# Float32 products in place of fp32r products of exact parts, in a two-layer attention and expert kernel

## The chip, the cores and the metric

One core of one Trainium2 chip. The metric is the device time of one execution in microseconds (us), as a median of runs. Nothing is computed on the host; weights lie in HBM as float32.

## The reference

Two layers over 256 latent tokens and 256 context tokens of width 1024, all in float32. Each layer mixes tokens, then sends them through experts:

```python
h = modulate(x, sh1, sc1); hc = modulate(xc, csh1, csc1)     # adaLN: shift, scale from SiLU(c) @ w_ada
p = h @ w_in[l]                     # 1440 columns: q rank 384 | kv rank 256 | rotary key 32 | GLU 512 | pool 256
q = rms_norm(p_q) @ w_uq            # 8 heads of 64 + 32
k, v = rms_norm(p_kv) @ w_ukv
attn = softmax(q k^T) v             # latent queries see context and latent keys
conv = silu(layer_norm(conv31(glu(p_conv)))); pool = window means @ pool_w
x = layer_norm(alpha * x + g1 * (concat(attn, conv, pool) @ w_out[l]))
combine = top-1 of 4 groups, then top-2 of its 8 experts     # 32 experts
for e in range(32):
    y += combine[:, e] * ((silu(h2 @ w_gate[e]) * (h2 @ w_up[e])) @ w_down[e])
x = layer_norm(alpha * x + g2 * y)
```

The second layer does not update the context tokens, so there half of the tokens go through mixing and experts (`nq`, `nb` = 2 tiles of 128 tokens instead of 4).

## The kernel before

The kernel is written on a tile framework. For VectorE (V), ScalarE (S, ACT in the profile), GpSimd (G, POOL) and the DMA queue on SyncE (SP) the framework's planner puts the instructions in an order, from their priority in the program and its own estimate of durations; some places are pinned by hand (`tc.issue_after(instruction)`, `tc.high_priority`). In the expert loops TensorE's order is as written (`manual_schedule`).

**Weights.** `plan` lists every weight transfer in the order of use. `pump` (L175) issues the next one on SP's queue as soon as a place of 1 MB is free. `RING` = 6 places are there from the start; others are added as buffers fall free (`slot`): in layer 0 one tile `w` and four `c` tiles at the start of the experts (L1508, L1740), in layer 1 the second half of the tokens, two `early` tiles, `k2`, two `c` tiles, two `w` tiles, `cr` and `misc`.

**Exact parts.** Outside attention's scores and the expert weights, products run on fp32r. To keep accuracy both sides are split into a high part (rounded to fp32r) and a low part (what the rounding left), and three products are added: high x high, high x low, low x high. `wsplit` (L386) makes the parts of a weight in one of two `w` buffers: a copy on ACT (L395), a subtraction on VectorE or, where `SPG` says so, POOL (L401). `mm3` (L406) and L465 to L467, L793, L807 to L809 do the triples. Tokens are split in `tokens_T` (L446, L447) and L525 to L537, the normed low ranks in `rms_T` (L714, L715), the pieces of the mix at L763, L866, L952.

**Mixing** (`mixing`, L369). Layer 0 has 512 columns of tokens, layer 1 has 256. `proj_block` (L461) makes one of six blocks of 128 channels with eight triples. `lowrank` (L666) makes q and kv ranks, in layer 0 already with plain float32 products (L674), in layer 1 with triples of 288 and 384 columns. The convolution is 31 taps for each of two blocks on VectorE (L607), part of the second block on ACT and POOL (`conv_part`). `rms_T` squares on ACT, takes the root on POOL (L262), scales on VectorE (L703) and turns the result on TensorE (L711). `k_pair`, `q_pair` and the value product follow, then eight heads: scores L884 (float32), softmax, turns L919, values L941. The output projection `out_part` (L958) runs in four parts, halves of columns by halves of channels, each with 4 channel blocks for each token tile; `merge`, `stats`, `rows_T` and `logits` (L1095) follow, then the router on VectorE (L1204 to L1276). `exact` (L1159) writes the tokens to DRAM for the gathers and splits them (L1170, L1171).

**Experts** (`moe`, L1306). 16 pairs of experts in quads of two pairs; each expert takes up to 64 tokens. `slots` (L1345) finds which token is in which place. `gather` brings the tokens of a quad: for the first quad a product of the tokens' two parts with the one-hot table (L1396), for the others an indirect DMA and turns (L1392). `half` (L1416) multiplies gate and up for the two experts of a pair side by side on 64 columns of the array each, in plain float32; `hidden` (L1424 to L1426) the gate; `down` (L1460) the output, also float32. `weighted` (L1448) scales it and splits it into `O`'s two parts (L1450, L1451). `scatter` (L1465) brings two pairs back to one tile of tokens and one half of the columns, a *unit*: four fp32r products with the table `gt` (L1474), the gate (L1477), the sum on POOL or VectorE (L1478). The units of a quad are spread over the next quad's loop. A branch (`tc.If`, L1608) holds passes for experts with more than 64 tokens; layer 1 has one such pass built in (`one_pass`). Ahead of the branch in layer 0 two rows are scaled on POOL (L1506).

## Time and profile before

| what | value |
|---|---|
| median of 3 runs | 1072.38 us (1064.46 to 1073.56) |
| profiled execution, its own time | 1077.6 us |
| its span, first to last instruction | 1075.9 us |
| mean granted TensorE clock | 0.939 of full speed |
| read from HBM | 309.03 MB |

Stretches are given in us from the span's start. Layer 0 mixes until about 263, routes until about 332 and runs its experts until 600; layer 1 mixes until about 737, projects and routes until 802 and runs its experts to the end. PE is TensorE, DVE VectorE. A record of a matmul has a start and a modelled end that overlaps the next one, so the cost of one is read from start to start. A float32 product leaves two records in the trace, an fp32r product one.

### The profile page before, as it was taken

The page shows a single profiled execution, that of the slowest core. Times are in us where ns is not written, and L with a number is a line of the kernel's source. Part 1 is how long each engine was busy: PE and PEld are TensorE (multiplying, and loading weights), DVE is VectorE, ACT ScalarE, POOL GpSimd, SP SyncE. Part 2 cuts the span into 40 slices and gives each one's busy share as a digit, 9 for nine tenths or more (in the row PEclk, how much of TensorE's full clock was granted, in tenths as well). Part 3 has the DMA queues.
Part 4 walks back from the last instruction along what each step waited for, and adds up shares of the span by engine and source line. Part 5 has one row for each costly group of instructions (what it writes and reads, how often), then busy time and mean ns, then how long its engine had stood idle before and what let it go on. Part 6 is the DMA issues. An engine that isn't in the chain of part 4 may idle for free. (4 is left out here: it accounts for less than half of the span.)

```text
span 1075.9 us, 13982 instructions
## 1 busy us (share of the span) xinstructions
PE 952.6 (89%) x5153; PEld 553.3 (51%) x5153; DVE 604.5 (56%) x1157; ACT 303.6 (28%) x598; POOL 317.2 (29%) x280
## 2 busy tenths in 40 slices
PE   4996999999668999999999888898859997999994
PEld 2674586687543454445444687646633443443442
DVE  2599567757844344455344899877572333433336
ACT  2432365532401111111111536443212221221211
POOL 2334510002361334324234632102070122123222
PEclk8898899999888999999999999999769998998997
DMA  9844225865979999999998677265768999999971
GB/s 356 324 157 161 80 79 204 326 120 178 348 263 318 329 395 406 402 376 380 381 400 320 217 236 256 99 240 178 270 207 302 396 387 392 393 400 407 381 250 41
DMA packets 95530, 305.41 MB, mean 284 GB/s; under 512 B 10247, under 2 KB 30727, under 8 KB 87392
## 3 DMA queue, kind: packets, MB, share of 16 engines
q1 hardware_dynamic: 89744, 293.77, 74.9%
q0 software_dynamic: 4272, 6.14, 1.7%
q10 hardware_dynamic: 1440, 4.54, 1.1%
q8 instruction: 43, 0.70, 0.3%
q14 instruction: 31, 0.25, 0.1%
HBM read 309.03 MB, written 4.72 MB: 292 GB/s over the span
## 5 line engine op out<-in xcount | busy, mean ns | idle before, releaser
L1478 POOL TENSOR_TENSOR x<-x,tm 128x512 f32<-128x512 f32 x96 | 122.8, 1298 | 309.5 <-DVE tm L1477 309.1
L1416 PE MATMUL gu<-ring,xt 128*64 128x512 f32 x504 | 172.8, 624 | 0.0
L1416 PE MATMUL gu<-slot,xt 128*64 128x512 f32 x416 | 133.6, 612 | 0.0
L1451 DVE SCALAR_TENSOR_TENSOR O<-d,iw,O 128x512 fp32r<-128x512 f32 x63 | 47.2, 749 | 123.8 <-ACT O L1450 122.8
L1474 PE MATMUL y<-O,gt 128*128 128x512 f32 (+2 forms) x400 | 110.1, 412 | 4.2 <-DVE tm L1477 3.4
L1474 PEld LDWEIGHTS y<-O,gt 128*128 128x128 f32 (+1 forms) x400 | 70.7, 192 | 51.3 <-issue 25.9
L1477 DVE TENSOR_TENSOR tm<-y,lnb 128x512 f32<-128x512 f32 (+1 forms) x102 | 68.9, 677 | 46.3 <-PE y L1474 44.8
L1416 PEld LDWEIGHTS gu<-ring,xt 128*64 128x64 f32 x504 | 49.7, 143 | 67.9 <-issue 63.7
L1450 ACT ACTIVATE O<-d,iw 128x512 fp32r<-128x512 f32 x63 | 43.3, 688 | 140.5 <-PE d L1460 139.5
L1460 PE MATMUL d<-ring,ht 128*64 128x512 f32 x264 | 82.7, 597 | 0.2 <-DMA ring<-in_w_down_dram 0.2
L607 DVE SCALAR_TENSOR_TENSOR c0b<-c0a,hw,c0b 128x256 f32<-128x256 f32 (+1 forms) x105 | 73.6, 747 | 0.6
L1425 DVE SCALAR_TENSOR_TENSOR hd<-th,gu 128x256 f32<-128x256 f32 x32 | 13.5, 421 | 91.4 <-ACT th L1424 91.1
L1416 PEld LDWEIGHTS gu<-slot,xt 128*64 128x64 f32 x416 | 38.5, 140 | 50.9 <-issue 47.5
L395 ACT ACTIVATE w<-ring 128x1024 fp32r<-128x1024 f32 (+2 forms) x42 | 41.0, 978 | 66.4 <-PE p L409 47.4
L1460 PE MATMUL d<-slot,ht 128*64 128x512 f32 x168 | 52.7, 595 | 0.0
L401 DVE TENSOR_TENSOR w<-ring,w 128x1024 fp32r<-128x1024 f32 (+2 forms) x33 | 39.7, 1205 | 22.1 <-ACT w L395 21.9
L1375 POOL DMA_INDIRECT xg<-h2d,ix x28 | 32.9, 1174 | 52.6 <-DVE ix L1374 24.4
L296 PE MATMUL p<-ring,scw 128*32 128x256 f32 x672 | 45.1, 404 | 2.3 <-DMA ring<-in_w_ada_dram 2.3
L1424 ACT ACTIVATE th<-gu 128x256 f32<-128x256 f32 x32 | 12.3, 385 | 108.8 <-PE gu L1416 108.8
L408 PE MATMUL p<-w,mix 128*128 128x512 f32 x96 | 38.6, 402 | 4.9 <-DVE w L401 4.9
L1460 PEld LDWEIGHTS d<-ring,ht 128*64 128x64 f32 x264 | 24.2, 137 | 33.6 <-issue 31.1
L1392 PEld LDWEIGHTS x<-ident,xg 128*128 128x128 f32 x224 | 29.5, 192 | 21.2 <-issue 18.7
(424 smaller groups left out, 1876.5 us busy)
## 6 DMA issues: line engine op xcount, KB each, us to landing
ring<-in_w_ada_dram SPq DMA_DIRECT2D x46, 1024.0 KB, 7.7
ring<-in_w_down_dram SPq DMA_DIRECT2D x32, 1024.0 KB, 11.6
ring<-in_w_gate_dram SPq DMA_DIRECT2D x63, 512.0 KB, 13.3
ring<-in_w_up_dram SPq DMA_DIRECT2D x63, 512.0 KB, 9.9
slot<-in_w_gate_dram SPq DMA_DIRECT2D x54, 512.0 KB, 13.0
slot<-in_w_up_dram SPq DMA_DIRECT2D x54, 512.0 KB, 12.8
slot<-in_w_down_dram SPq DMA_DIRECT2D x21, 1024.0 KB, 14.8
ring<-in_w_in_dram SPq DMA_DIRECT2D x6, 1024.0 KB, 15.6
```

The lines of the kernel that those rows point to most:

```text
L296: T.matmul(ps[32 * q:32 * q + 32, :256], scw[:, j, 6 - 2 * k:38 - 2 * k], w[:, jj, q * 256:q * 256 + 256], start=(j == 0), stop=(j == 7), ...
L395: kept_hi.append(S.activation(h_, src, AF.Copy))
L401: ins = e.tensor_tensor(l_, src, h_.bitcast(FT), op=OP.subtract)
L408: T.matmul(ps, lh, rl, start=False, stop=False, skip_group_check=True)
L607: V.scalar_tensor_tensor(acc, tap(b, k), hw[:, b, k:k + 1], acc, op0=OP.mult, op1=OP.add)
L1416: T.matmul(gu[64 * s:64 * s + 64, :].rearrange("p (g c) -> p g c", g=2), xt[h][:, j % 4, o0 + 64 * s:o0 + 64 * s + 64], ws[s].rearrange("p ...
L1450: S.activation(oh, ps, AF.Copy, scale=w)
L1451: V.scalar_tensor_tensor(ol, ps, w, oh.bitcast(FT), op0=OP.mult, op1=OP.subtract)
L1460: T.matmul(ps[64 * s:64 * s + 64, :n], ht[:, k, 64 * s:64 * s + 64], ws(s, k, c, n), start=(k == 0), stop=(k == 1), skip_group_check=True, ...
L1474: T.matmul(ps, GT[key][r, t * 128:(t + 1) * 128], O[key][k][r, c], start=(i == 0 and k == 0), stop=(i == m - 1 and k == 1))
L1477: V.tensor_tensor(tm, ps, gates[t // 2][hf][:, c0:c0 + n], op=OP.mult)
L1478: eng.tensor_tensor(x[:, t, cols], x[:, t, cols], tm, op=OP.add)
```

## The change

All fp32r tiles become float32 tiles and every triple, and every pair with a split side, becomes one float32 product. `wsplit`, `mm3`, `proj_w` and all low parts go; weights are read where the DMA put them, and a place is given back when the products on it are done. The key product runs as two 64-column halves side by side. The scaled tokens of layer 0 are made on ACT and VectorE in turn; every second low-rank piece is scaled on VectorE. The pins of `mixes(1)`, `conv_part` and of the late splits go. `RING` is 8; in layer 0 two `c` tiles become places already after attention and two more with the experts; layer 1 gets one `early` tile, and `c0a` at the experts, but no `w` tile. The scaling at L1506 moves from POOL to ACT. `info` has four columns instead of six.

```diff
-RING = 6
+RING = 8
...
-            def wsplit(src, n, eng=None, late=0):
...
-            def mm3(ps, lh, ll, rh, rl, start, stop):
-                T.matmul(ps, lh, rh, start=start, stop=False, skip_group_check=True)
-                T.matmul(ps, lh, rl, start=False, stop=False, skip_group_check=True)
-                T.matmul(ps, ll, rh, start=False, stop=stop, skip_group_check=True)
...
-                    T.matmul(ps[:, :NQ], wh[:, j, :], hTh[j][:, :NQ], start=(j == 0), stop=False)
-                    T.matmul(ps[:, :NQ], wh[:, j, :], hTl[j][:, :NQ], start=False, stop=False)
-                    T.matmul(ps[:, :NQ], wl[:, j, :], hTh[j][:, :NQ], start=False, stop=(j == 7))
+                    T.matmul(ps[:, :NQ], src[:, j, c * 128:(c + 1) * 128], hT[j][:, :NQ], start=(j == 0), stop=(j == 7))
...
-            with tc.issue_after(kept_lo[0].ins):
-                mixes(1)
-            with tc.issue_after(kept_hi[-CP].ins) if CP else nullcontext():
-                conv_part(1, 0, CONV1[l])
+            mixes(1)
+            conv_part(1, 0, CONV1[l])
...
-                    for n, (x1, x2) in enumerate(((wkh, kT[j][0]), (wkh, kT[j][1]), (wkl, kT[j][0]))):
-                        T.matmul(ps, x1[:, j, cols], x2, start=(j == 0 and n == 0), stop=(j == 1 and n == 2))
+                    for e in range(2):
+                        T.matmul(ps[64 * e:64 * e + 64, :], w[:, j, 2 * hp + e, 0:64], kT[j], start=(j == 0), stop=(j == 1),
+                                 skip_group_check=True, tile_position=(0, 64 * e))
...
-                        mm3(ops[hf][t], mixh[b][:, t * 128:(t + 1) * 128], mixl[b][:, t * 128:(t + 1) * 128],
-                            wh[:, k, :], wl[:, k, :], bi == 0 and b2 == 0 and k == 0,
-                            bi == 1 and b2 == 1 and k == 1)
+                    T.matmul(ops[hf][t], mix[4 * bb + k][:, t * 128:(t + 1) * 128], w[:, k, :],
+                             start=(bi == 0 and k == 0), stop=(bi == 1 and k == 3), skip_group_check=True)
...
-                S.activation(hh, h2, AF.Copy)
-                (G if t % 2 else V).tensor_tensor(hl, h2, hh.bitcast(FT), op=OP.subtract)
...
-                        for k, h2 in enumerate((h2h, h2l)):
-                            T.matmul(ps[:, jj * 256:jj * 256 + n], h2[t][:, 128 * j:128 * j + 128], g[:, t, :n],
-                                     start=(t == 0 and k == 0), stop=(t == nb - 1 and k == 1), skip_group_check=True)
+                        T.matmul(ps[:, jj * 256:jj * 256 + n], h2[t][:, j::8], g[:, t, :n],
+                                 start=(t == 0), stop=(t == nb - 1), skip_group_check=True)
...
-                S.activation(oh, ps, AF.Copy, scale=w)
-                V.scalar_tensor_tensor(ol, ps, w, oh.bitcast(FT), op0=OP.mult, op1=OP.subtract)
+                S.activation(o, ps, AF.Copy, scale=IW[key][:, 6:7])
...
-                        for k in range(2):
-                            r, c = (slice(0, 128), cols) if key != "o" else (slice(64 * hf, 64 * hf + 64), slice(0, 512))
-                            T.matmul(ps, GT[key][r, t * 128:(t + 1) * 128], O[key][k][r, c],
-                                     start=(i == 0 and k == 0), stop=(i == m - 1 and k == 1))
+                        r, c = (slice(0, 128), cols) if key != "o" else (slice(64 * hf, 64 * hf + 64), slice(0, 512))
+                        T.matmul(ps, GT[key][r, t * 128:(t + 1) * 128], O[key][r, c], start=(i == 0), stop=(i == m - 1))
...
-                    G.tensor_scalar(t_, t_, ALPHA, None, op0=OP.mult)
+                    S.activation(t_, t_, AF.Copy, scale=ALPHA)
```

## Rows read from the trace of the kernel before

**Rows 1.** The page, busy time of each engine, share, instructions.

```profile
PE 952.6 (89%) x5153; PEld 553.3 (51%) x5153; DVE 604.5 (56%) x1157; ACT 303.6 (28%) x598; POOL 317.2 (29%) x280
```

**Rows 2.** Stretches: length, busy time of five engines, PE clock, DMA share, GB/s.

```profile
0.00:130.00 130.00, 101.48 (x604) 69.14 (x605) 83.84 (x116) 41.79 (x85) 51.90 (x54) 0.89 0.59 215
130.00:263.00 133.00, 132.54 (x800) 97.34 (x799) 89.49 (x183) 60.87 (x132) 8.71 (x10) 1.00 0.58 184
263.00:332.00 69.00, 46.32 (x369) 31.76 (x369) 47.26 (x83) 17.48 (x24) 37.09 (x27) 0.83 0.86 307
332.00:600.00 268.00, 256.88 (x1230) 121.61 (x1227) 116.88 (x215) 44.83 (x90) 95.95 (x80) 1.00 0.99 371
600.00:737.00 137.00, 122.24 (x790) 94.09 (x788) 117.40 (x227) 68.40 (x135) 34.87 (x30) 0.96 0.59 202
737.00:802.00 65.00, 45.31 (x242) 32.81 (x241) 45.60 (x105) 14.11 (x18) 24.91 (x27) 0.76 0.70 226
802.00:1076.00 274.00, 247.80 (x1128) 106.55 (x1128) 104.04 (x230) 56.12 (x117) 63.73 (x55) 0.93 0.86 329
```

**Rows 3.** PE's waits, 332 to 600 us: total, times, longest.

```profile
PE y L1432 <- DVE hd L1426: 7.5, 6, 1.3
PE y L1432 <- DMA slot<-in_w_up_dram: 1.2, 1, 1.2
```

**Rows 4.** PE's waits, 0 to 130, 263 to 332, 600 to 802, 802 on.

```profile
PE p L711 <- DVE t L703: 12.2, 1, 12.2
...
PE y L1345 <- PEq L1608: 5.5, 1, 5.5
PE p L1235 <- DVE t L1229: 4.7, 1, 4.7
...
PE p L408 <- DVE w L401: 8.8, 5, 4.9
PE y L1345 <- DVEq L1608: 8.6, 1, 8.6
...
PE x L1396 <- DVE t L1263: 3.6, 1, 3.6
...
PE x L1387 <- DMA xo<-h2d,ix: 5.7, 1, 5.7
```

**Rows 5.** PE's timeline (start, length, what), scores of head 0.

```profile
162.49 1.88 PE L884 MATMUL p<-c1b,c0b 128*128 128x512 f32 x4
164.20 1.03 PE L889 MATMUL p<-c1b,c0b 128*128 128x256 f32 x4
```

**Rows 6.** PE's timeline, output projection of layer 0, first product and what follows.

```profile
229.88 0.48 PE L407 MATMUL p<-w,mix 128*128 128x512 f32 x1
...
262.89 1.95 PE L1084 MATMUL p<-ident,x 128*128 128x128 f32 x16
```

**Rows 7.** PE's timeline, two scatter units and what follows.

```profile
368.42 2.10 PE L1474 MATMUL y<-O,gt 128*128 128x512 f32 x8
370.46 3.65 PE L1416 MATMUL gu<-slot,xt 128*64 128x512 f32 x16
```

**Rows 8.** PE's timeline, second half of the first gather.

```profile
302.19 4.10 PE L1396 MATMUL x<-g,h 128*128 128x256 f32 x32
306.12 0.95 PE L1345 MATMUL y<-info,g 128*128 128x6 f32 x8
```

**Rows 9.** DVE's timeline ahead of L703.

```profile
98.41 2.35 DVE L401 TENSOR_TENSOR w<-ring,w 128x1024 fp32r<-128x1024 f32 x2
100.68 6.70 DVE L607 SCALAR_TENSOR_TENSOR c0b<-c0a,hw,c0b 128x512 f32<-128x512 f32 x10
```

**Rows 10.** Timelines of DVE and POOL around the routers and the branch.

```profile
285.81 1.99 DVE L1171 TENSOR_TENSOR h<-hn,h 128x1024 fp32r<-128x1024 f32 x1
...
305.70 5.93 POOL L1506 TENSOR_SCALAR lnb<-lnb 128x1024 f32<-128x1024 f32 x2 [7.92 <-DMA lnb<-in_rpack_dram]
...
779.69 2.97 DVE L1247 TENSOR_TENSOR g<-iot,pos 128x512 fp32r<-128x512 f32 x1
```

More of the change, by code (lines that the diff above doesn't have):

```diff
@@ L1 @@
 import math
-from contextlib import ExitStack, nullcontext
+from contextlib import ExitStack
 import concourse.bass as bass
@@ L265, in big @@
     def big(tag, shape, dt, name):
-        return per.tile(shape, dt, tag=tag, name=name, bufs=2 if tag == "w" else 1)
+        return per.tile(shape, dt, tag=tag, name=name)
     def blocks(tags, n, m, dt, name):
@@ L472, in mixing @@
             if l == 0:
-                kt2 = big("k2", [128, 4, 512], FT, "xT")
-                xT = [kt2[:, k, :] for k in range(4)] + [cv1[0][:, 1152:1664], cv1[1][:, 1088:1600], cv0[1][:, 512:1024], t2(FT)]
+                xT = blocks("k2 w", 8, 512, FT, "xT")
                 for j in range(8):
@@ L830, in mixing @@
                 conv(1)
-                mixh[4:6], mixl[4:6] = (blocks(b, 2, NQ, FR, "mix") for b in ("b0d", "b1d"))
             cst = sb.tile([128, 4, 6], FT, tag="cst", name="cst")
@@ L963, in out_part @@
                 w = get(("out", l, hf, bb))
-                parts = [wsplit(w[:, 2 * b2:2 * b2 + 2, :], 1024, V, LATE[l] if hf + bi == 0 else 0) for b2 in range(2)]
-                order = [(b2, t) for b2 in range(2) for t in range(nq)]
+                order = [(k, t) for k in range(4) for t in range(nq)]
                 if hf == 1 and bi == 1:
-                    order = [(b2, t) for t in range(nq) for b2 in range(2)]
-                for b2, t in order:
-                    if each and b2 == 0:
+                    order = [(k, t) for t in range(nq) for k in range(4)]
+                for k, t in order:
+                    if each and k == 0:
                         each(t)
-                    wh, wl = parts[b2]
-                    for k in range(2):
-                        b = 4 * bb + 2 * b2 + k
-                        mm3(ops[hf][t], mixh[b][:, t * 128:(t + 1) * 128], mixl[b][:, t * 128:(t + 1) * 128],
-                            wh[:, k, :], wl[:, k, :], bi == 0 and b2 == 0 and k == 0,
-                            bi == 1 and b2 == 1 and k == 1)
+                    T.matmul(ops[hf][t], mix[4 * bb + k][:, t * 128:(t + 1) * 128], w[:, k, :],
+                             start=(bi == 0 and k == 0), stop=(bi == 1 and k == 3), skip_group_check=True)
                 done(("out", l, hf, bb))
@@ L1051, in mixing @@
                         e.tensor_tensor(xs, xs, lg_[1][hf], op=OP.add)
+            else:
+                held_.extend(big(c, [128, 2048], FT, "slot") for c in ("c1a", "c1b"))
+                for t_ in held_:
+                    slot(t_)
             gate = [bc_row(dA, G1 + s) for s in range(ns)]
@@ L1133, in mixing @@
             if l:
-                for k in range(2):
-                    slot(big("w", [128, 2048], FT, "slot"))
-            if l:
                 behind(nq)
@@ L1505, in moe @@
                     row_to_all(t_, a["rpack"][l, :, 2, :], r, 0, 4)
-                    G.tensor_scalar(t_, t_, ALPHA, None, op0=OP.mult)
-            if not last:
-                more_ = [big("w", [128, 2048], FT, "slot")]
-                slot(more_[0])
+                    S.activation(t_, t_, AF.Copy, scale=ALPHA)
             def hot(q):
@@ L1731, in moe @@
                 one_pass()
-            if last:
-                XG = big("c0a", [128, 2, D], FT, "xg")
-                XG = [XG[:, k, :] for k in range(2)]
-                kept["xo"] = big("c1a", [128, D], FT, "xo")[0:64, :]
-                G.memset(kept["xo"], 0.0)
-            else:
-                XG = [big(b, [128, D], FT, "xg") for b in ("b0b", "b1b")]
-                more_ += [big(c, [128, 2048], FT, "slot") for c in ("c0a", "c0b", "c1a", "c1b")]
-                for t_ in more_[1:]:
-                    slot(t_)
+            XG = big("c1a" if last else "b0a", [128, 2, D], FT, "xg")
+            XG = [XG[:, k, :] for k in range(2)]
             for k in range(2):
                 G.memset(XG[k], 0.0)
-            ohs, ols = (blocks(b, 3, D, FR, "O") for b in ("b0d b0a", "b1d b1a"))
+            if last:
+                kept["xo"] = big("b1b", [128, D], FT, "xo")[0:64, :]
+                G.memset(kept["xo"], 0.0)
+                slot(big("c0a", [128, 2048], FT, "slot"))
+            else:
+                held_.extend(big(c, [128, 2048], FT, "slot") for c in ("c0a", "c0b"))
+                for t_ in held_[2:]:
+                    slot(t_)
+            os_ = blocks("b0d b1d b0b", 3, D, FT, "O")
             order.enter_context(tc.manual_schedule(engines={mybir.EngineType.PE}))
@@ L1793, in moe @@
                     done(("wd", l, e))
[L1794 removed]
+                O[i] = o_
                 if not odd:
```

239 lines of the change are left out of this document (77 added, 162 removed).

## The prediction

> **What bounds the kernel now.** I read the page's busy line first, then the table of stretches, then what TensorE waited for in each stretch, and last the order of its instructions inside the stretches. TensorE is busy 89% of the span and no other engine is above 56% [rows 1]. The average hides stages, so [rows 2] cut the span where the work changes. From 130 to 263 us (layer 0: keys, queries, attention, output projection) TensorE has 132.5 of 133 us: whatever it is given there moves the end one for one. From 332 to 600 us (layer 0 experts) it has 256.9 of 268 at full clock, and from 802 us on (layer 1 experts and the end) 247.8 of 274. In those stretches the DMA queues look just as full (0.99 and 0.86), and the reader must decide which of the two paces them: in layer 0's experts TensorE waited 7.5 us for the hidden rows on VectorE and only 1.2 us for a weight [rows 3]. So TensorE paces them, and the DMA fills because slots come free at TensorE's pace. The four other stretches hold nearly all idle time of TensorE: 28.5 us before 130, 22.7 from 263 to 332, 14.8 from 600 to 737, 19.7 from 737 to 802, each the length less the busy time of its row in [rows 2]. The large waits in them [rows 4] are for VectorE or for the branch at L1608, not for data.
>
> **The price of a product.** The change swaps groups of fp32r products for one float32 product, so all hangs on what each costs start to start. Row L884 shows the float32 form on a full 128x128 tile with 512 columns: four records, which are two calls by the code, take from 162.49 to 164.20 us [rows 5], so 0.857 us a call. A triple of fp32r products (L407 to L409) costs less: the 48 triples of the last three quarters of the output projection run from 229.88 to 262.89 us [rows 6], 0.688 us each. So one float32 call for a triple is +0.17 us at 512 columns. At 256 I take half of both, +0.085 us.
>
> The scatter is worse off, because there the pair of exact parts stood on one side only. Two units of L1474, eight fp32r calls, take from 368.42 to 370.46 us [rows 7], 1.02 us a unit of four calls. Afterwards a unit is two float32 calls, 1.71 us: +0.69. The gather of the first four experts (L1396): 32 calls from 302.19 to 306.12 us [rows 8], 0.246 us a pair; one float32 call of 256 columns is half of 0.857, 0.43: +0.18.
>
> The Trainium skill ("FP8 and Floating Point Precision", section "TensorE Precision Notes") says that true FP32 takes four passes through the array. Counted in passes against one for a reduced product, a scatter unit would go from 4 to 8, twice its 1.02 us, and the 96 units would cost 98 us instead of the 66 below. The rows speak for the smaller sum: fp32r calls run slower than a quarter of the float32 call here (0.255 us against 0.214), and the float32 call has been seen in this very shape.
>
> **The change part by part.** *0 to 130 us.* Six projection blocks of eight products: 48 x 0.17 = +8.2 us. But TensorE then waits 12.2 us for L703 [rows 4]. VectorE reaches L703's square sums late because it first runs two splits (2.35 us) and ten convolution taps (6.70 us) [rows 9]. The splits go; the taps stay. So TensorE's lateness falls into a wait that itself shrinks by little more than the splits: I take -2 us; the bounds are +8 (the taps are ordered later too) and -8 (they move behind L703).
>
> *130 to 263 us.* 24 query, 16 key and value and 64 output triples: 104 x 0.17 = +17.7 us. The new key product runs as two column halves side by side, for the same 0.857. Nothing comes back: there was no idle time. The splits of weights that go from ACT and VectorE were hidden by TensorE's own work here, so in this stretch they are worth nothing.
>
> *263 to 332 us.* Gather: 32 x 0.18 = +5.9. Gone from the path of the router's mask: 1.99 us of the L1171 subtraction on VectorE [rows 10], for which L1235 waited in its 4.7 us [rows 4]. Gone from POOL: the scaling L1506, 5.93 us just ahead of the branch [rows 10], on which the 5.5 us wait at L1345 hangs; ACT is free there and does it in less, so I take 3.4 us. Sum +0.5 us. Bounds: +10 (the first gather follows a pause in a stretch with a mean clock of 0.83 [rows 2], where its cost may double) and -4 (both waits, 4.7 and 5.5 us, go altogether, against the +5.9).
>
> *332 to 600 us.* Eight quads, each with eight scatter units (four token tiles, two halves): 64 x 0.69 = +44.2 us. The removed low part (L1451 on VectorE) was hidden. The waits for hidden rows stay, since what covers them does not change. Ring of eight, earlier slots: they hide transfers that cost TensorE 1.2 us, so nothing; if they came late, the cost would be those waits. Bounds +30 (the hidden-row waits vanish and the planner packs better) and +48.
>
> *600 to 802 us.* 48 triples of 512 columns, 8.2; 120 of 256 to 384 columns, at 0.085 to 0.12, 11; 16 gathers, 2.9: +22 us. Against it: waits for the low parts, 8.8 us [rows 4]; about 3 us of shorter waits on the high parts and tokens; the 3.6 us wait ahead of L1396, behind VectorE's 2.97 us one-hot table [rows 10], which shared its time with POOL's half of L1171; about 2 us of the 8.6 us at the branch; and some 3 us because TensorE then idles less and its clock (0.76 from 737 to 802 [rows 2]) falls less. That is 20.4 us, an estimate from these rows; I take 0 for the net. Bounds -12 and +20: 34.5 us of idle time stood in this stretch.
>
> *802 us to the end.* 32 units, 22.1 us. Back: 1.4 us of the 5.7 us wait for the extra pass's rows [rows 4], since two longer units stand in front of it, and about 1 us of smaller waits. +20 us. Bounds +14 and +24.
>
> **The sum.** -2 + 17.7 + 0.5 + 44.2 + 0 + 20 = +80 us. The profiled execution took 1077.6 us (span 1075.9), so 1158 by its own time; it lies 5.2 us above the median of the runs, 1072.4. Forecast for the median: 1153 us.
>
> **The rivals.**
> *Relief larger.* VectorE and ACT lose all splits, and the four stretches with idle time give back 25 us more than counted: the tap wait, the branch and mask waits. 1153 - 25 = 1128 us. For it: 85.7 us of idle time in these stretches. Against: most of it is waiting for taps, masks, branches and first data, which stay. Chance 0.2.
>
> *Order lost.* The lists of who does what, the pins that go (the mixes, the taps and the late splits were held behind named instructions), and the planner's order on VectorE, ACT and POOL were made for the old costs. If the taps again run ahead of what TensorE needs, the waits of 12.2 and 8.6 us stay or grow: +20, 1173 us. For it: [rows 9] show such an order already. Against: every removed instruction can only thin VectorE's line. Chance 0.12.
>
> *DMA paces the experts.* If from 332 us and from 802 us the transfers set the pace, TensorE's 66 us of longer scatters vanish behind them, and three more places let some 3 MB land earlier, at the 371 GB/s of [rows 2] 8 us more: 1153 - 66 - 8 = 1079 us, within 1% of before: not slower. It decides once TensorE waits for weights in each pair. For it: DMA shares of 0.99. Against: the 1.2 us of [rows 3]. Chance 0.03.
>
> **How the numbers follow.** The forecast has 0.65, larger relief 0.2, lost order 0.12, DMA pace 0.03. The forecast's own bounds are about 1135 to 1166. The range reaches toward the relief and the lost order until 2 in 10 are out: 1124 to 1172. About 1% is what a measurement of this kernel can tell from no change. Only the DMA case ends near it, with 0.02 inside 1% and 0.01 below: faster 0.01, same 0.02, slower 0.97.
>
> **What would show it.** Right: L1474 with half its calls but two records each, a unit at about 1.71 us; the layer 0 expert stretch about 44 us longer with TensorE busy as before; the stretch of attention and output projection about 18 us longer; the two router stretches no longer. Wrong: a scatter unit at 1.02 us or at 2.04; TensorE waiting for w_gate or w_down in every pair; or a wait ahead of L711 above 12 us.

## The result and the profile after

The changed kernel takes 1158.49 us (median of 4 runs, 1153.13 to 1159.67); the kernel before, run on the same chip beside it, 1070.74 us. The ratio is 1.0819, with a 95% interval of 1.0758 to 1.0879: slower, 5.5 us above the forecast and inside its range. The profiled execution took 1158.72 us (span 1157.1). The profiled execution before, at 1077.6 us, is one of the longest of its kernel: so the two profiles lie 81 us apart and the two medians 88.

The page's busy line of the kernel after answers to [rows 1]: VectorE, ACT and POOL lose work (VectorE 129 us of it), and TensorE gains 120 us with fewer instructions.

```profile
PE 1072.4 (93%) x4963; PEld 532.9 (46%) x4963; DVE 475.1 (41%) x1016; ACT 240.6 (21%) x524; POOL 262.3 (23%) x253
```

The table of stretches of the kernel after, cut where the same work begins: at the first pooling product, the first router row that is turned (L997), the first down product (L1354), the second block of layer 1's turned tokens, and the placing products behind layer 1's branch. The columns are those of [rows 2].

```profile
0.00:129.20 129.20, 107.41 (x554) 60.51 (x555) 67.51 (x104) 29.46 (x65) 38.66 (x45) 0.93 0.61 224
129.20:279.70 150.50, 150.50 (x713) 77.50 (x712) 74.07 (x164) 48.42 (x120) 7.13 (x9) 1.00 0.55 176
279.70:358.65 78.95, 64.73 (x385) 46.00 (x385) 39.05 (x80) 12.41 (x23) 23.14 (x20) 0.78 0.72 245
358.65:691.90 333.25, 319.99 (x1360) 137.08 (x1357) 100.37 (x198) 52.67 (x100) 97.09 (x84) 1.00 0.87 309
691.90:866.80 174.90, 162.33 (x798) 101.90 (x797) 114.23 (x275) 42.46 (x101) 33.76 (x43) 0.97 0.61 209
866.80:1157.10 290.30, 267.43 (x1158) 109.95 (x1158) 79.85 (x196) 55.21 (x117) 62.52 (x52) 0.96 0.83 314
```

The same events in the kernel before lie at 129.3, 262.9, 332.15, 615.8 and 802.0 us. The forecast's stretches meet a little ahead of the fourth of them, at the first block of turned tokens (600.64 us before, 679.31 after), and the next table is cut there.

Its last three columns split the change up. "Work" is TensorE's busy time, with what it did at the lower of its two clock levels (1.2 GHz) counted half; "lower level" is the other half; "idle" is the rest of the stretch. This is an estimate from the busy time and the granted clock of both traces: TensorE did 82.7 us of its work at the lower level before and 58.7 after, and 16 equal records that take 1.87 us at the upper level take 3.46 at the lower (shown below).

| stretch | before | after | change | forecast | work | lower level | idle |
|---|---|---|---|---|---|---|---|
| projections and low ranks, layer 0 | 129.3 | 129.2 | 0 | -2 | +8.9 | -2.2 | -6.7 |
| attention and output projection, layer 0 | 133.6 | 150.5 | +16.9 | +17.7 | +17.4 | 0 | -0.5 |
| router and first gather, layer 0 | 69.3 | 79.0 | +9.7 | +0.5 | +9.0 | +9.2 | -8.5 |
| experts, layer 0 | 268.5 | 320.7 | +52.2 | +44.2 | +51.3 | 0 | +0.9 |
| mixing and router, layer 1 | 201.4 | 187.5 | -13.9 | 0 | +19.3 | -12.5 | -20.6 |
| experts and end, layer 1 | 273.9 | 290.3 | +16.3 | +20 | +26.0 | -6.4 | -3.3 |

The sum is +81 against +80, but three stretches missed by eight to fourteen microseconds, not all in one direction. What has to be explained is not the total.

TensorE's timeline of the kernel after, at the row that answers to [rows 7], with the placing products (`slots`, now L1242) behind it:

```profile
452.03 3.70 PE L1367 MATMUL y<-O,gt 128*128 128x512 f32 x8
455.57 0.60 PE L1289 MATMUL x<-ident,xg 128*128 128x128 f32 x4
456.01 2.15 PE L1242 MATMUL y<-info,g 128*128 128x4 f32 x16
458.09 0.65 PE L1354 MATMUL d<-slot,ht 128*64 128x512 f32 x2
```

The eight records are two scatter units of two float32 calls each, from 452.03 to 455.57: 1.77 us a unit, where the forecast had 1.71 and where the row before had 1.02. And L1242, which the forecast did not price at all, needs two records a call where it had one: the eight calls for four experts take 2.08 us (456.01 to 458.09), and took 1.24 us before (451.53 to 452.77).

TensorE's waits in the kernel after that answer to [rows 4]: 0 to 130 us, then the stretch from 279.7 to 358.65, then 679 to 880 us, then the rest.

```profile
PE p L646 <- DVE t L638: 8.6, 1, 8.6
...
PE y L1328 <- DVE hd L1322: 4.4, 1, 4.4
PE p L1008 <- ACT hT L1002: 3.1, 1, 3.1
...
PE y L1242 <- PEq L1495: 2.2, 1, 2.2
...
PE y L1242 <- DVEq L1495: 5.8, 1, 5.8
...
PE x L1284 <- DMA xo<-h2d,ix: 3.5, 1, 3.5
```

Every wait of [rows 4] became shorter, and the waits for low parts are gone. One wait is new: L1008, the router's first logits, for ACT's copy of a router row.

### The profile page after: what moved, and what is told of

Its sections match the earlier page's. It is cut to its first block, busy times and chain, and to the rows that moved or that the text cites. A ratio compares the mean times of both kernels' runs of the same rounds, so it can differ in the third digit from the quotient of the medians.

```text
span 1157.1 us, 13273 instructions
## 1 busy us (share of the span) xinstructions
PE 1072.4 (93%) x4963; PEld 532.9 (46%) x4963; DVE 475.1 (41%) x1016; ACT 240.6 (21%) x524; POOL 262.3 (23%) x253
## 5 line engine op out<-in xcount | busy, mean ns | idle before, releaser
L1312 PE MATMUL gu<-ring,xt 128*64 128x512 f32 x696 | 201.4, 620 | 0.0
L1367 PE MATMUL y<-O,gt 128*128 128x512 f32 (+2 forms) x400 | 182.0, 595 | 5.1 <-DVE tm L1369 4.2
L1354 PE MATMUL d<-slot,ht 128*64 128x512 f32 x232 | 74.3, 596 | 0.0
L1354 PE MATMUL d<-ring,ht 128*64 128x512 f32 x208 | 74.2, 595 | 0.0
L553 DVE SCALAR_TENSOR_TENSOR c0b<-c0a,hw,c0b 128x256 f32<-128x256 f32 (+1 forms) x105 | 71.1, 718 | 1.6
L1345 ACT ACTIVATE O<-d,iw 128x512 f32<-128x512 f32 x63 | 43.3, 687 | 135.5 <-PE d L1354 134.5
L1312 PE MATMUL gu<-slot,xt 128*64 128x512 f32 x192 | 71.3, 610 | 0.0
L884 PE MATMUL p<-ring,mix 128*128 128x512 f32 x160 | 69.5, 593 | 0.0
L425 PE MATMUL p<-hT,ring 128*128 128x512 f32 (+1 forms) x192 | 66.7, 505 | 3.0 <-ACT hT L481 2.4
L425 PEld LDWEIGHTS p<-hT,ring 128*128 128x128 f32 x192 | 37.0, 196 | 30.3 <-issue 22.6
L884 PEld LDWEIGHTS p<-ring,mix 128*128 128x128 f32 x160 | 30.1, 190 | 36.3 <-issue 35.1
L1302 DVE TENSOR_SCALAR xt<-x,chan 128x256 f32<-128x256 f32 x32 | 16.7, 539 | 61.7 <-PE x L1289 57.1
L1354 PEld LDWEIGHTS d<-ring,ht 128*64 128x64 f32 x208 | 22.0, 137 | 35.0 <-issue 34.3
## 6 DMA issues: line engine op xcount, KB each, us to landing
slot<-in_w_down_dram SPq DMA_DIRECT2D x28, 1024.0 KB, 11.3
```

The source lines that it names most:

```text
L425: T.matmul(ps[:, :NQ], src[:, j, c * 128:(c + 1) * 128], hT[j][:, :NQ], start=(j == 0), stop=(j == 7))
L553: V.scalar_tensor_tensor(acc, tap(b, k), hw[:, b, k:k + 1], acc, op0=OP.mult, op1=OP.add)
L884: T.matmul(ops[hf][t], mix[4 * bb + k][:, t * 128:(t + 1) * 128], w[:, k, :], start=(bi == 0 and k == 0), stop=(bi == 1 and k == 3), skip_ ...
L1312: T.matmul(gu[64 * s:64 * s + 64, :].rearrange("p (g c) -> p g c", g=2), xt[h][:, j % 4, o0 + 64 * s:o0 + 64 * s + 64], ws[s].rearrange("p ...
L1345: S.activation(o, ps, AF.Copy, scale=IW[key][:, 6:7])
L1354: T.matmul(ps[64 * s:64 * s + 64, :n], ht[:, k, 64 * s:64 * s + 64], ws(s, k, c, n), start=(k == 0), stop=(k == 1), skip_group_check=True, ...
```

## The experiments

The table gives four stretches of each profile, cut at events that every version has: A from the first turned router row to the first down product (layer 0's router and gather), B to the first of layer 1's turned tokens (layer 0's experts), C to layer 1's first down product (its mixing and router), D to the end. Times are medians; the kernel before took 1068.7 to 1070.7 us beside them. The stretches are those of one profiled execution each, for the kernel before the one of 1077.6 us.

| kernel | time | A | B | C | D |
|---|---|---|---|---|---|
| before | 1070 | 69.3 | 268.5 | 214.1 | 261.1 |
| after | 1158.5 | 78.9 | 320.7 | 200.4 | 277.4 |
| after, placing on fp32r | 1152.7 | 78.4 | 317.5 | 200.5 | 275.8 |
| after, scatter by one fp32r product | 1074.9 | 79.0 | 257.9 | 204.5 | 256.0 |
| after, ring of six | 1163.6 | 78.8 | 326.5 | 204.2 | 277.8 |
| before, scatter in float32 | 1143.0 | 70.0 | 319.6 | 208.4 | 281.6 |
| before, layer 1's mixing in float32 | 1057.3 | 68.7 | 268.1 | 198.9 | 257.4 |
| the same, idle splits put back | 1072.7 | 69.4 | 269.4 | 211.8 | 257.2 |
| before, row scaling on ACT | 1072.2 | 75.3 | 268.0 | 211.6 | 257.4 |
| after, router rows copied by VectorE | 1156.9 | 78.4 | 320.7 | 200.7 | 279.0 |
| after, tokens kept in blocks of channels | 1155.5 | 79.6 | 320.5 | 198.9 | 276.5 |
| before, layer 1's mixing in float32, key rows by ACT | 1056.3 | 71.1 | 269.4 | 203.6 | 261.1 |

### The scatter alone

```diff
-    V.scalar_tensor_tensor(ol, ps, w, oh.bitcast(FT), op0=OP.mult, op1=OP.subtract)
...
-    for k in range(2): T.matmul(ps, GT[key][r, ...], O[key][k][r, c], ...)
+    T.matmul(ps, GT[key][r, ...], O[key][0][r, c], ...)
```

> The kernel before, with the scatter alone in float32 (no low part of the experts' outputs, one-hot table as float32). Theory of the forecast: 96 units of two calls at 1.71 instead of four at 1.02 us, +66, less 2 to 3 us of waits in layer 1: 1071 + 64 = 1135 us, of which 44 lie in layer 0's experts. Theory 'the whole of the experts' loss is the scatter': layer 0's experts alone lengthen by the 50 us seen in the changed kernel and the sum is about +70, 1141 us. Rival 'removed VectorE work gives back': under +50, 1120 us or less.

Measured: 1142.99 us, ratio 1.0678 (1.0637 to 1.0719). Stretch B grows by 51.1 us and D by 20.5; C, which has no edit in it, falls by 5.7 with less work at the lower clock level (25.1 us instead of 38.5). So the scatter alone carries the experts' whole loss in the changed kernel (B +52.2), as the second theory had it. Two units take 3.54 us here too (447.80 to 451.34 us), so 64 units at 1.77 instead of 1.02 make 48; the rest is in the waits of this stretch (TensorE's waits, 332.28 to 651.88 us, of this experiment):

```profile
PE y L1432 <- DVE hd L1426: 8.8, 7, 1.3
PE y L1472 <- DVE tm L1474: 4.2, 2, 2.4
PE y L1345 <- DVE tm L1474: 2.9, 5, 0.6
```

The PSUM bank `y` comes free only when VectorE has taken the last unit's sum out of it (`tm`); the kernel before lost 0.9 us there.

In D the estimate of the result's table goes further than the times do: TensorE did 15.7 us of its work there at the lower level in the profile of before, 12.6 in this one and 3.4 in the changed kernel. With half of that taken off, D grows by 22.0 us here and by 22.3 in the changed kernel.

### The placing products

```diff
-    T.matmul(pi[:, :4], g[:, t, c0:c0 + 128], infov[:, t, :], ...)      # g, info float32
+    T.matmul(pi[:, :6], g[:, t, c0:c0 + 128], infov[:, t, :], ...)      # g, info fp32r, exact parts
```

> The changed kernel, with the placing products (`slots`, 96 calls with 4 columns) back on fp32r with exact parts (6 columns); everything else as changed. Theory 'the small products were left out of the sum': each of these calls takes about 0.23 us as float32 (two records, two weight loads) and 0.12 us as fp32r, and they stand on TensorE's own path in both expert stretches, so 96 x 0.11 = 11 us go: 1147 us, about 7 us of them from 358 to 692 us and 4 behind 867 us. Rival 'small products hide in waits': the time stays within 3 us of 1158, because TensorE waits for hidden rows anyway.

Measured: 1152.68 us (1152.37 to 1153.27), 5.8 below the changed kernel, half of what was expected. In stretch B, TensorE's busy time falls from 308.6 to 303.3 us, which is nearly the expected amount, but the stretch shortens by only 3.1. TensorE's waits in it tell where the rest went:

```profile
PE y L1330 <- DVE hd L1324: 8.8, 7, 1.3
PE y L1244 <- DVE tm L1371: 2.9, 5, 0.6
```

The faster placing products arrive at the bank `y` before VectorE has emptied it: 2.9 us that the changed kernel doesn't have. So the small products were missing from the sum, and part of their price stood in front of another wait.

### One fp32r product for the scatter: who paces the experts

```diff
-    os_ = blocks("b0d b1d b0b", 3, D, FT, "O")      # gt float32 as well
+    os_ = blocks("b0d b1d b0b", 3, D, FR, "O")      # gt fp32r as well
```

> The changed kernel, with the scatter as one fp32r product per pair (0.255 us a call instead of about 0.88); this leaves out the low part of the experts' outputs. Theory 'TensorE paces the experts': 64 units of two calls fall from 1.77 to 0.51 us, -81 us in layer 0, and 32 units give -38 us in layer 1: about 1039 us, with waits for hidden rows as before. Rival 'the DMA paces as soon as TensorE is a little faster': the 103 MB of layer 0's expert stretch can't go faster than the 374 GB/s that the kernel before showed at full queues (359 GB/s at 0.96), so that stretch ends at 275 us instead of 252, and TensorE waits for w_gate or w_down in most pairs: 1060 us or more.

Measured: 1074.88 us; the experts of layer 0 (B) end at 257.9 us instead of 320.7. The row of that stretch, in the form of [rows 2]:

```profile
357.15:615.06 257.91, 235.52 (x1152) 103.99 (x1149) 93.28 (x188) 46.50 (x90) 97.32 (x82) 1.00 1.01 383
```

TensorE's longest waits in the same stretch:

```profile
PE y L1329 <- DVE hd L1323: 13.7, 14, 1.3
PE y L1368 <- DVE tm L1370: 1.9, 4, 0.9
PE y L1368 <- DVE mvx L359: 1.7, 1, 1.7
PE y L1329 <- DMA ring<-in_w_up_dram: 1.2, 1, 1.2
```

Neither theory has it whole. The stretch is 10.6 us shorter than in the kernel before, whose queues already stood at 0.99, and waits for weights are 1.2 us in all: the full queues of [rows 2] did not pace the kernel. TensorE's busy time falls by 73 us (a call takes 0.26 to 0.28 us where 0.255 was expected), and 10 of these come back as idle time, chiefly the wait for hidden rows: it is met 14 times, for less work now stands in front of it. How much more than 383 GB/s the queues would give was not tried. In layer 1's experts D is 21 us shorter, where 38 were expected: 35 us of busy time go and 14 come back as idle time, chiefly in the waits for hidden rows (6.1 us instead of 1.2) and for the extra pass's rows (6.6 instead of 3.5); waits for weights are about 3 us.

### The ring of six

```diff
-RING = 8
+RING = 6
```

> The changed kernel with a ring of six places instead of eight. Theory 'TensorE paces, the ring is worth nothing': 1158 us, within 3 us either way. Rival 'the ring pays': two places of 1 MB less in flight cost some 5 to 8 us at the starts of the stretches (2 to 3 MB at 371 GB/s), seen as TensorE waiting for ring places in the first 130 us or at the first pairs of a layer.

Measured: 1163.55 us, 5.1 more than with eight places. The "ring pays" side is right in size. Stretch B is 5.8 us longer, with this wait in it that the kernel with eight places doesn't have:

```profile
PE d L1354 <- DMA ring<-in_w_down_dram: 2.9, 2, 2.1
```

The forecast gave the ring nothing because the kernel before, with six places, lost 1.2 us to weights. The diff has a reason why six would no longer do: the buffer `w` is single now, and the slot that the kernel before took from it in layer 0's experts (`more_`) is gone. That link was argued from the diff, not tried alone. The 2.9 us are half of what the stretch loses; the other half is longer busy time, in part at the lower clock level, which was granted from 393.9 to 397.3 us, just behind the wait.

### Layer 1's mixing alone

```diff
-    wh, wl = w_ or proj_w(src, c)
+    if l: T.matmul(ps[:, :NQ], src[:, j, c * 128:(c + 1) * 128], hTh[j][:, :NQ], ...)
...
-    hTt = [[big(b + p, [128, n, 512], FR, "hT") ...] for b in ("b0", "b1")]
+    hTt = [[big(b + p, [128, n, 512], FT if l else FR, "hT") ...] for b in ("b0", "b1")[:2 - l]]
```

The same is done for the low ranks, keys, values, queries, heads and output projection of layer 1, and layer 1's pins of `mixes(1)` and `conv_part` go, as in the change.

> The kernel before, with layer 1's mixing (projections, low ranks, keys, values, queries, output projection) on unsplit float32 and no split of its weights, tokens or heads; layer 0, gather, placing and scatter of both layers stay on fp32r with exact parts. Theory 'relief': the 11 us that the changed kernel gained between the turned tokens and the first pair of layer 1's experts come from the splits that stood in TensorE's way there; this kernel gains them alone, 1071 - 11 = 1060 us. Rival 'the price stays': 48 products of 512 columns and 120 of 256 to 384 are dearer by 19 us, and the waits for low parts give 9 back: 1081 us. Rival 'it came from elsewhere' (the ring, layer 0): within 3 us of 1071.

Measured: 1057.33 us, ratio 0.9899 (0.9872 to 0.9926): 1% faster than the kernel before, clear of the interval. Stretch C falls from 214.1 to 198.9 us. The row of C in the kernel before, in the form of [rows 2]:

```profile
600.64:814.77 214.13, 178.16 (x1064) 130.54 (x1064) 166.10 (x343) 83.00 (x156) 63.21 (x61) 0.89 0.61 203
```

The same row of this experiment:

```profile
597.58:796.45 198.87, 179.39 (x913) 110.75 (x912) 128.54 (x305) 53.00 (x116) 42.98 (x52) 0.96 0.65 219
```

TensorE's busy time moves by 1.2 us, although the forecast priced the dearer products there at 19. The granted clock is the reason to be read here: 0.89 before and 0.96 now. Of TensorE's work in this stretch the kernel before did 38.5 us at the lower of the two levels, this one 11.3, with 19.5 us of idle time instead of 36.0. Counted as in the result's table, the dearer products cost 14.8 us of work here (19 were priced), the lower level gives back 13.6 and idle time 16.5. The share of the clock is the loose one of these. Two other experiments run the instructions of the kernel before in C, the scatter alone and the row scaling: C takes 208.4 and 211.6 us there, with 25.1 and 31.5 us of work at the lower level and 37.8 and 37.6 us of idle time. So the clock gives back between 7 and 14 us here, by the execution that one compares with.

### The splits as idle work

The kernel above, with layer 1's weight splits issued again, their results read by nobody:

```diff
     if l:
+        proj_w(src, c)
         T.matmul(ps[:, :NQ], src[:, j, c * 128:(c + 1) * 128], hTh[j][:, :NQ], ...)
...
+    if l: wsplit(w[:, 2 * jq:2 * jq + 2, :], 2 * width)
```

> The kernel before with layer 1's mixing in float32, as in the earlier run at 1057 us, but with the splits of layer 1's weights put back as work that nothing reads: the same ACT copies and VectorE or POOL subtractions at the same places (tokens and heads stay unsplit). Theory 'TensorE waited for the parts': without a reader the splits hold TensorE up nowhere, and the time stays within 3 us of 1057. Rival 'the engines were too full': ACT and VectorE are as late as before with everything else behind them, and 8 us or more of the 11 come back: 1065 us or more.

Measured: 1072.67 us. All of the gain is gone, 13 us of it in stretch C, though no product waits for a part. The rival holds: it is the load of the splits on ACT, VectorE and POOL together. Of the 13 us, 9.6 are idle time; the other 3.5 come from more work at the lower level (18.3 us instead of 11.3), which is no more than that level varies by. VectorE's timeline of this experiment ahead of the key rows of layer 1 (L704), where TensorE then waits 9.0 us:

```profile
644.02 2.35 DVE L401 TENSOR_TENSOR w<-ring,w 128x1024 fp32r<-128x1024 f32 x2
646.29 7.21 DVE L606 SCALAR_TENSOR_TENSOR c0b<-c0a,hw,c0b 128x256 f32<-128x256 f32 x18
653.42 0.95 DVE L401 TENSOR_TENSOR w<-ring,w 128x768 fp32r<-128x768 f32 x1
...
658.29 1.66 DVE L704 TENSOR_SCALAR t<-p,ss 128x256 f32<-128x256 f32 x4 [0.92 <-POOL ss L262]
```

Without the splits, in the kernel at 1057 us, the same place reads:

```profile
632.33 13.69 DVE L605 SCALAR_TENSOR_TENSOR c0b<-c0a,hw,c0b 128x256 f32<-128x256 f32 x29
...
647.24 1.66 DVE L701 TENSOR_SCALAR t<-p,ss 128x256 f32<-128x256 f32 x4 [1.14 <-POOL ss L262]
```

The key rows come 49.7 us after C begins (at 597.58) instead of 58.5 (at 599.81). VectorE stands in one line of convolution taps and splits, and what TensorE needs next stands at the end of it. What the copies on ACT and the subtractions on POOL add to this was not tried apart.

### The scaling of the norm rows

```diff
-    G.tensor_scalar(t_, t_, ALPHA, None, op0=OP.mult)
+    S.activation(t_, t_, AF.Copy, scale=ALPHA)
```

> The kernel before, with the scaling of layer 0's two norm rows (L1506) on ACT instead of POOL, nothing else. Theory of the forecast: the branch ahead of the second quad's placing products stands behind 5.9 us of POOL work, so its 5.5 us wait gives back about 3.4 us: 1067 us. Rival 'the branch waits for VectorE's count or for the engines' common wait': the wait stays at 5 us or more, and the time within 1 us of 1071.

Measured: 1072.2 us, ratio 1.0038 (1.0015 to 1.0061): not faster, rather 4 us slower. The wait at the branch stays at 5.5 us, so the rival is right about the wait, though the time is not within its 1 us. Stretch A is 6.0 us longer in this profile, but 3.3 of these arise ahead of the edit's place: the lower clock level was granted from 267.5 to 274.3 us, in the router's logits, where the profile of before has the upper one. TensorE's two longest waits in the router's stretch of this experiment:

```profile
PE y L1432 <- DVE hd L1426: 8.6, 1, 8.6
PE y L1345 <- PEq L1608: 5.5, 1, 5.5
```

The first of them was 6.7 us before. VectorE's timeline shows it: the hidden rows (L1425, L1426) are ordered behind a row product (L1487) that takes 6.37 us here, and 1.22 a little earlier in the same profile.

```profile
317.47 1.22 DVE L1486 TENSOR_TENSOR x<-x,lnb 128x1024 f32<-128x1024 f32 x1
...
318.95 6.37 DVE L1487 TENSOR_TENSOR x<-x,lnb 128x1024 f32<-128x1024 f32 x1
325.25 2.56 DVE L1359 TENSOR_SCALAR gt<-iot,iw 128x512 fp32r<-128x512 f32 x1
327.73 0.41 DVE L1425 SCALAR_TENSOR_TENSOR hd<-th,gu 128x256 f32<-128x256 f32 x1
```

From 319.59 to 327.52 us POOL is in row products of the same kind (2.35, 2.34 and 3.21 us).

### The new wait in the router

```diff
-ROWS = ('SS', 'VV')
+ROWS = ('VS', 'VV')
```

> The changed kernel, with the first half of layer 0's router rows copied out of PSUM by VectorE instead of ACT (the copies in front of the 3.1 us wait of the first logits). Theory 'a new wait and the clock after it': the 3.1 us wait goes and the half clock behind it (about 3.3 us more for the logits and the modulation products that follow) goes with it: 1158 - 6 = 1152 us. Rival 'the wait moves': VectorE stands in its own line of row products, the copy comes as late, and the time stays within 2 us of 1158.

Measured: 1156.85 us (1153.87 to 1160.51), within the spread of the changed kernel: inconclusive in the time, and the profile says why. TensorE's timeline of the changed kernel behind the wait:

```profile
284.76 2.72 PE L1008 MATMUL p<-wb,hT 128*128 128x36 f32 x16 [3.09 <-ACT hT L1002]
...
291.04 3.46 PE L1008 MATMUL p<-wb,hT 128*128 128x36 f32 x16
294.44 3.64 PE L292 MATMUL p<-ring,scw 128*32 128x256 f32 x32
...
299.61 1.87 PE L1008 MATMUL p<-wb,hT 128*128 128x36 f32 x16
301.42 1.93 PE L292 MATMUL p<-ring,scw 128*32 128x256 f32 x32
```

TensorE's timeline of this experiment, from the wait to the first pair's hidden rows:

```profile
285.16 1.12 PE L1008 MATMUL p<-wb,hT 128*128 128x36 f32 x8 [3.14 <-DVE hT L1000]
...
310.78 10.52 PE L1292 MATMUL x<-g,h 128*128 128x256 f32 x32 [2.70 <-DVE t L1169]
...
351.61 0.67 PE L1328 MATMUL y<-ident,hd 128*128 128x128 f32 x2 [5.62 <-DVE hd L1322]
```

In the changed kernel the same 16 records take 3.46 us soon after the wait and 1.87 later. After a pause of 3.1 us TensorE ran at the lower of its two levels (1.2 GHz); the trace has the granted clock there from 285.8 to 299.4 us. In the experiment the wait is still 3.1 us, now for VectorE, but the low level behind it is shorter (286.1 to 292.9 us; the granted clock from 279 to 300 us is 0.84 instead of 0.67), and the mask's products come 27.5 us after the stretch's start instead of 30.0. These 2.5 us are lost again: the first gather takes 10.5 instead of 9.5 us and the hidden rows are waited for 5.6 instead of 4.4.

### The gather's weight load

```diff
-    T.matmul(ps[:, ...], h2[t][:, j::8], g[:, t, :n], ...)
+    T.matmul(ps[:, ...], h2[t][:, 128 * j:128 * j + 128], g[:, t, :n], ...)
```

> The changed kernel, with the gather of the first four experts taking 128 neighbouring channels as its stationary side instead of every eighth; this leaves the channels of those four experts' tokens in another order than their weights. Theory 'the strided weight load is the price': its 338 ns falls to the 190 ns of the other full loads, and a call from 0.493 us to 0.43: 32 calls give 2 us in layer 0, and the 8.05 us stretch of 16 calls becomes 6.9. Rival 'clock or VectorE': the 16 calls stay at about 8 us, whatever the load.

Weight loads of the gather in the changed kernel (duration in ns: least, median, most; first and last start):

```profile
L1292 PEld LDWEIGHTS x<-g,h x96: 312/338/339, 312.9 to 859.6; 128*128 128x128 f32 x96
```

The same loads in the experiment, and the 16 calls of the second half of the first gather in both kernels, the changed one first:

```profile
L1292 PEld LDWEIGHTS x<-g,h x96: 186/190/337, 312.2 to 849.4; 128*128 128x128 f32 x96
...
325.92 8.05 PE L1292 MATMUL x<-g,h 128*128 128x256 f32 x32
...
324.51 7.17 PE L1292 MATMUL x<-g,h 128*128 128x256 f32 x32
```

Measured: the 16 calls of the second half of the first gather take 7.01 us (324.51 to 331.52) instead of 7.89 (325.92 to 333.81), 0.44 us a call instead of 0.493. The first theory holds for the call. This kernel ran once, in 1149.55 us, with a stretch A of 72.4 us, 6.5 less; the calls of both halves of the gather explain 1.5 of that, and the rest lies in the waits and in less work at the lower clock level (23.6 us instead of 31.5). A single execution doesn't tell whether that comes with the edit. The kernel before had made its tokens' parts in contiguous blocks of channels; the change dropped that copy and reads every eighth channel. That a stride of 32 bytes is dear fits the Trainium skill ("SBUF — State Buffer", section "Door 1: The DMA port swizzle (why `[64,N]` ≈ `[32,N]`)"), which says that SBUF is read in lines of 16 bytes and that only consecutive accesses to one line run at full speed; the two rows agree with it.

The next run keeps the values and makes the blocks contiguous where the tokens are written:

```diff
+    o_ = h2[t].rearrange("q (j p) -> q j p", j=8)[:, :, 64 * hf:64 * hf + 64]
+    x_, g_, b_ = (v.rearrange("q (p j) -> q j p", j=8) for v in (x[:, t, cols], ga[...], be[...]))
+    V.tensor_tensor(o_, x_, g_, op=OP.mult)
```

> The changed kernel with the tokens' copy for the gather kept in another order of channels (128 neighbours belong to one block), so that the gather's and the later turns' stationary or moving slices are contiguous; the values are the same. Theory 'the strided weight load is the price of the router stage': loads at 190 instead of 338 ns, 16 calls in 7.2 instead of 8.05 us, and the stretch from the router to the first down product 4 to 6 us shorter, as the look with wrongly ordered channels had it: 1153 us. Rival 'the cost only moves': VectorE and ACT read strided rows instead, their row products become longer ahead of the router's chain, and the time is 1158 or more.

Measured: 1155.52 us (1154.88 to 1156.71). The second half of the gather falls to 7.02 us as expected, but stretch A is 79.6 us, not shorter: the strided rows cost VectorE more (45.7 us busy in it instead of 39.1), the wait of the first logits grows from 3.1 to 4.0 and that for hidden rows from 4.4 to 5.5. In layer 0 the cost only moved. The 3 us in the total are not told apart from the spread of the runs.

### The faster kernel, and the wait that kept the first stretch

The kernel with layer 1's mixing in float32, with layer 0's key rows scaled by ACT, so that they no longer stand behind the taps:

```diff
-VA = (['KR1', 'KR2', 'KP', 'R2', 'R3', 'Z'], ...)
+VA = (['KR1', 'KR2', 'KP', 'R3', 'Z'], ...)
-    V.tensor_scalar(ss[:, :nb], ...)
+    (G if l == 0 and nj == 2 else V).tensor_scalar(ss[:, :nb], ...)
```

> The kernel before with layer 1's mixing in float32, and with layer 0's key rows scaled by ACT (L703 and its one small operand on POOL) instead of VectorE. Theory 'the ten convolution taps make the 12.2 us wait': past them the wait falls to about 3 us, so 8 to 9 us less than 1057: 1048 us. Rival 'other work is late next' (the taps, ACT's rows): the wait comes back as another one before 145 us, within 2 us of 1057.

Measured: 1056.27 us (1050.72 to 1061.53), ratio 0.9856 (0.9824 to 0.9889). TensorE's wait at that place:

```profile
PE p L709 <- ACT t L703: 4.8, 1, 4.8
```

It was 12.2 us, and layer 0's router begins 6.2 us earlier (254.7 instead of 260.8 us): VectorE's line ahead of the key rows, two splits and ten taps in [rows 9], did make this wait. This run moves the rows past both. That the taps are enough shows in the changed kernel, which has no splits: there VectorE runs 17 taps in the same place, and TensorE waits 8.6 us. VectorE's timeline of the changed kernel, then the key rows of the kernel before:

```profile
96.69 11.59 DVE L553 SCALAR_TENSOR_TENSOR c0b<-c0a,hw,c0b 128x512 f32<-128x512 f32 x17
...
109.52 1.66 DVE L638 TENSOR_SCALAR t<-p,ss 128x256 f32<-128x256 f32 x4 [1.16 <-POOL ss L258]
...
109.06 1.66 DVE L703 TENSOR_SCALAR t<-p,ss 128x256 f32<-128x256 f32 x4 [0.95 <-POOL ss L262]
```

The median is only 1 us below the kernel without this edit, and the intervals overlap; in the profiled execution stretches A, C and D are longer by 2.4, 4.7 and 3.7 us. That is the clock: TensorE did 57 us of its work in A, C and D at the lower level in this profile and 31 in that of the kernel without the edit, and the first is the longest of its six executions, the second the shortest. D shows it without an edit in it. It takes 257.2 to 257.4 us in three versions of the kernel before, with 5.0 to 5.6 us of work at the lower level, and 261.1 in two, with 15.5 and 15.7; the profiled execution of before is one of these. Whole executions of the kernel before, beside the experiments, agree: it took under 1066.6 us where its mean granted clock was 0.951 to 0.959, and over 1072.4 where it was 0.939 to 0.950.

## Why the prediction was right, and where its steps failed

The forecast's mechanism, TensorE dearer by the price of the call in stretches that it fills, is shown: the scatter alone makes +73 us, attention and output projection +17. The small total error is partly luck. The forecast's prices add up to 120 us and it let 40 of them come back; the work in the result's table grows by 132 us, and 51 come back. The two errors are about the same size and cancel.

**130 to 263 us** (+17.7, seen +16.9): right. TensorE has no idle time there, and 48 products of the output projection run from 238.46 to 279.71 us, 0.859 us each where the price was 0.857. It is the one stretch with nothing to give back.

**The experts** (+44.2 and +20, seen +52.2 and +16.3): right in mechanism, too small in size. The mis-sized term is the unit in layer 0: 1.77 instead of 1.71 us, +4. The step "the removed low part was hidden" held. The placing products were absent from the sum: they cost 5.4 us of TensorE in layer 0, of which 3.1 show in the time. These two make up the 8 us. The ring, costed at nothing, brought no gain over the kernel before, but its eight places kept off a loss of 5.8 us that six would have brought. In layer 1 the work grows by 26 us where 22 were priced: the trace has the calls of 36 units there and not of 32, since the built-in extra pass adds some. Less work at the lower clock level gives 6 back, a term that the forecast did not have; with the clock set aside the scatter alone and the whole change agree there (22.0 and 22.3 us).

**The four-pass rule** weighed in the forecast would have made a unit 2.04 us. With 1.77 and 0.859, the sum from rows was the nearer one.

**0 to 130 us** (-2, seen 0): right in mechanism. Dearer products fell into the wait for the key rows (12.2 to 8.6 us). But that wait did not shrink by the splits: VectorE reaches the key rows at 109.5 us, and did at 109.1 before, since it now runs 17 taps where two splits and ten taps stood. Only TensorE's later arrival shortened it.

**263 to 332 us** (+0.5, seen +9.7): failed. Three steps did it. "One float32 call of 256 columns is half of 0.857" gave 0.43; it is 0.493, because the stationary side is strided now, and the two halves of the gather together take 17.3 us instead of 9.5, +7.8 where 5.9 was priced. "Gone from POOL: the scaling, so I take 3.4 us" is refuted: the scaling alone moved to ACT leaves the branch's wait as it was. By the rows, the wait's fall to 2.2 us in the changed kernel goes with TensorE arriving later, behind the dearer gather. And a new wait of 3.1 us with the lower clock level behind it was not foreseen: TensorE did 31.5 us of its work here at the lower level where it had done 13.2, which makes 9.2 us, about as much as idle time gives back (8.5). What the new wait alone costs was not settled, since removing part of it was given back two waits later.

**600 to 802 us** (0, seen -13.9): the rival "Relief larger" named the right mechanism but expected it in other places. Three terms missed, all in one direction. The price is 19 us of work instead of 22. Idle time gives back 21 us where 17 were listed (8.8, 3, 3.6 and 2 us). And "some 3 us because TensorE then idles less and its clock falls less" is mis-sized: TensorE did 31.9 us of its work here at the lower level before and 6.8 after, which gives back 12.5, of which up to 7 can be the long execution of before. The listed waits also hide what they come from. They are where VectorE's lateness shows, not what it consists of: with the load put back and no reader, one new 9.0 us wait appears and 13 us return.

**Order lost**: against. The waits of 12.2 and 8.6 us fell to 8.6 and 5.8, although the taps do run ahead of the key rows again.

**DMA paces the experts**: against. With a shorter scatter the same queues carried the same weights in 258 instead of 268 us.

What stays open: what each single wait in layer 0's router costs, why the clock falls in one execution of a stretch and not in another, and whether the lost slot is what made six places too few.

## What to carry to other kernels

Price a swap of product forms per call from the very shape, then count all products of the swapped tensors, the tiny ones too, and look at the stride that the new operand has. Where TensorE has no idle time the price comes through whole. Where it idles, ask which engine's queue is the long one: here work that was removed outright (the splits of layer 1) gave back more than the waits that named it, and work moved from one engine's queue to another's gave back nothing that could be told from the spread (three runs). Read the granted clock of the same stretch too, in more than one execution: with the same instructions it moved a stretch by 4 to 6 us. In sum the change has two halves of opposite sign: layer 1's mixing gains 1% by unsplit float32, the scatter loses 7%.

## What the runs showed of the hardware that was not expected

A float32 weight load of 128x128 took 338 ns with every eighth element and 190 ns with neighbours, and with 256 columns moved the call's price went with it (0.493 against 0.44 us).

A float32 product with 4 columns took 0.26 us a call (2.08 us for eight), one of fp32r with 6 columns 0.155 us (1.24 for eight), with two records and one: with so few columns the price goes by records, 0.13 and 0.155 us each, and hardly by columns.

How much of its work TensorE does at the lower clock level moved times by as much as some of the edits did: in layer 1's mixing it was 25, 32 and 39 us in three executions of the same instructions, and 11 without the splits; in the last stretch, with the same instructions, 5 or 16 us, which makes 4 us of time.

VectorE's product of two 128x1024 tiles took 1.21 us in one place and 5.41 or 6.37 us while POOL was in products of the same kind; in the kernel before and in the one with the scaling on ACT the hidden rows of the first pair stand behind one of these. The Trainium skill ("SBUF — State Buffer", section "SBUF: two separate sides") says that the two engines hold a shared port exclusively for a whole instruction; these rows agree, without a run that separates them.
